# Both output projections and the down projection in seven half-size products with tokens stationary, the up projection in full products

## The chip, the cores and the metric

The kernel runs on one core of a Trainium2 chip. The metric is the device time of one execution in microseconds, here the median of three runs. A profile shows one further execution: its span is the time from its first to its last recorded instruction, and its own run time is a little longer. Line numbers (L385) are those of the kernel before, unless it is said that they are of the change.

## The reference

One decoder layer on 512 tokens of width 1024 with a memory of 256 tokens, all in float32. Three mixer branches (short convolution, stick-breaking attention, retention) are merged by gates; what the change touches is this:

```
merged = jnp.sum(gates * up, axis=2)
x = x + merged @ w_o[l]                      # 1024 x 1024
h = rmsnorm(x, norm_xa_g[l])
mem_n = rmsnorm(mem, norm_mem_g[l])
x = x + memory_attention(h, mem_n, w_xq[l], w_xkv[l], w_xo[l])   # ends in o @ w_out, 1024 x 1024
h = rmsnorm(x, norm_mlp_g[l])
x = x + squared_relu_mlp(h, w_up[l], w_down[l])                  # square(relu(h @ w_up)) @ w_down
return rmsnorm(x, final_g)
```

`w_up` is 1024 x 4096 and `w_down` 4096 x 1024.

## The kernel before, in words

**Numbers.** Every float32 operand is split in two parts, h (rounded) and l (the rest). A product is three matmuls that accumulate in PSUM: h by h, h by l, l by h (`mm3`, L234 to L236). `split` makes h on ScalarE (a cast) and l on VectorE (a subtraction); `parts_of` (L111, L112) does the same for a block of weights.

**Weights.** They come in blocks of 128 x 1024 (512 KB) on SyncE's DMA queue into `w_raw` (RAWS = 3 buffers), and their parts lie in `w_part` (WBUFS = 11 buffers). The class `Stream` loads and splits them in the order in which a list of items, `plan`, uses them, AHEAD = 2 steps before.

**Order of the work.** `run_plan` walks through `plan` and calls each item. The order of instructions on an engine is then set by the framework's list scheduler, which moves instructions between items as far as data, buffers and its own estimates allow; it is fixed when the kernel is built. On the chip each engine takes its instructions, and the DMAs that it issues, in that order. The loads of `x`, of the norm gains `g_bc` and of the memory rows `m_sb` are issued by ScalarE.

**PSUM.** Two pools of four banks: `mmps` (tag "mm") and `atps` (tag "at"). The transposes of a normed token tile (`norm_T`, L385: eight 128 x 128 in two "at" banks) use "at".

**Two kinds of product.** In `proj_t` the weights are stationary and 512 tokens stream; the result has channels in partitions. In `proj_m` the tokens are stationary and 512 weight columns stream; the result has tokens in partitions, so it can be added to `x`. `w_o`, `w_xo` and `w_down` go by `items_m`: two halves of 512 columns, four chunks of weights each, four token tiles in four "mm" banks; after the last chunk `add_x` (L836) adds each bank to `x`. This is 192 matmuls for `w_o`, 192 for `w_xo` and 768 for `w_down`, all 512 wide.

**Seven products.** `seven` (L290 to L308) multiplies 2 x 2 blocks with seven half-size products in place of eight (Winograd's form): sums and differences of weight blocks (`Seven.combo`, L137) and of token blocks (`Mixes`) are multiplied, and the products are added up. Here the weights are stationary and 256 tokens stream. It serves 12 of the 24 columns of gates and, of the up projection's 32 columns, all but the first U7 = 8: 12 pairs of columns with 84 matmuls 256 wide each.

**Stages around the change.** The gates of the third branch end in pairs of `seven`; each finished merged column is split into `mgs`. Then `reload_x` loads x again, `mem_norm` loads two tiles of memory, norms and transposes them (L354, L376, L385), and `proj_norm` runs `w_o`: first half of columns, then the second half token by token, with each token's norm (`norm_begin`, `norm_end`) and transposes behind its last sum. Keys and values of the memory follow, then cross-attention (`xa_scores`, `xa_transpose`, `xa_out`), whose result is split into `xo`; `proj_norm` runs `w_xo`; `first_up` starts the MLP. In four rounds `up7` makes eight columns of `u` and `items_m` multiplies them by 1024 rows of `w_down`. The last half of columns goes token by token, and `final` norms and stores each token tile (L1034).

```
pss[t] = mmps()
proj_m(pss[t], ws, a(), t, 0, 8)
...
dve.tensor_tensor(out=dst, in0=ps, in1=dst, op=ALU.add)
```

Of the kernel before, what the change touches and what calls it, by code (L numbers as in the profile page):

```python
# [33 lines left out]
RAWS, WBUFS, AHEAD = 3, 11, 2  # L34
G7, U7 = 12, 8
# [3 lines left out]
def trunk_kernel(ctx: ExitStack, tc: tile.TileContext, x, mem, par, rot, dqd, kdec, g_mix, g_xa, g_mem, g_mlp,  # L39
# [75 lines left out]
    class Plain:  # L115


        def __init__(self, t, c):
            self.loads = [(t, c)]
            self.steps = [lambda raw: parts_of(raw[0])]  # L120
            self.parts = []
# [3 lines left out]

    class Seven:


        def __init__(self, t, c):
            self.loads = [(t, c), (t, c + 1)]  # L130
            self.steps = [self.s0, self.s1, self.s2, self.s3]
            self.parts = []

        def combo(self, a0, a1, b0, b1):
            x = wpool.tile([P, CW], F32, name="w_mix", bufs=2)
            dve.tensor_tensor(out=x[:, :512], in0=a0, in1=a1, op=ALU.subtract)
            dve.tensor_tensor(out=x[:, 512:], in0=b0, in1=x[:, :512] if b1 is None else b1, op=ALU.subtract)  # L137
            return x
# [4 lines left out]
        def s1(self, raw):  # L143
            ra, rb = raw
            self.x1 = self.combo(ra[:, 512:], ra[:, :512], rb[:, :512], ra[:, 512:])
            return parts_of(self.x1)

        def s2(self, raw):
            rb = raw[1]
            return parts_of(self.combo(rb[:, :512], self.x1[:, :512], rb[:, 512:], None))  # L150
# [8 lines left out]

    class Stream:  # L160
        def __init__(self, entries):
            self.loads = [l for e in entries for l in e.loads]
            self.steps, first = [], 0
            for e in entries:
                e.first = first
                for i, st in enumerate(e.steps):
                    self.steps.append((e, st, first + (len(e.loads) if i else 1)))
                first += len(e.loads)
                e.last = len(self.steps)
# [33 lines left out]
    def run_plan():  # L203
        entries, index = [], {}
        for chunks, _ in plan:
            for kind, t, c in chunks:
# [6 lines left out]
        for chunks, fn in plan:  # L213
            es = [index[(t.tensor.name, c)] for _, t, c in chunks]
            if es:
                done = max([done] + [e.last for e in es])
                st.pump(done + AHEAD)
            fn(*[e.get() for e in es])
# [28 lines left out]

    class Mixes:
# [7 lines left out]
        def make(self, g):  # L256
# [13 lines left out]
            mix("S3", scr("mix", (P, 2, 256)), a11, a21, ALU.subtract)  # L270
            mix("S1", a21, a21, whole(4, 256), ALU.add)
            mix("S2", a11, a21, a11, ALU.subtract)
# [9 lines left out]
    def seven(b, a):  # L282
# [11 lines left out]
        s, u, y1, y2 = scr("sv_s"), scr("sv_u"), scr("sv_1"), scr("sv_2")  # L294
        lo, hi = slice(0, 256), slice(256, 512)
        prod(p1, "A11", "B11", True)
        act.copy(out=s[:, lo], in_=p1[:, lo])  # L297
        prod(p3, "S1", "T1", True)
        act.copy(out=s[:, hi], in_=p3[:, lo])
        prod(p1, "S2", "T2", False)  # L300
        act.copy(out=u[:, lo], in_=p1[:, lo])
        prod(p2, "A12", "B21", True)
        dve.tensor_tensor(out=y1[:, lo], in0=p2[:, lo], in1=s[:, lo], op=ALU.add)
        prod(p1, "S3", "T3", False)
        act.copy(out=u[:, hi], in_=p1[:, lo])
        dve.tensor_tensor(out=y2[:, hi], in0=s[:, hi], in1=u[:, hi], op=ALU.add)
        prod(p3, "S4", "B22", False)
        dve.tensor_tensor(out=y2[:, lo], in0=p3[:, lo], in1=u[:, lo], op=ALU.add)  # L308
        prod(p1, "A22", "T4", False)
        return y1, p1, y2  # L310
# [40 lines left out]
    def sumsq(src, c, ss, dst):  # L351

        cs = slice(c * 512, (c + 1) * 512)
        act.activation(out=dst[:, cs], in_=src[:, cs], func=AF.Square, accum_out=ss[:, c:c + 1])  # L354
# [7 lines left out]
    def norm_begin(key, src):  # L362
# [4 lines left out]
        sumsq(src, 0, ss, S["xn", key])  # L367
# [3 lines left out]
    def norm_end(key, src, g_bc):  # L371

        xn, ss = S["xn", key], S.pop(("ss", key))
        sumsq(src, 1, ss, xn)
# [347 lines left out]
    def gated(n, d, ps2, gt):  # L722
# [8 lines left out]
        if n == 2:  # L731
            if d % 2 == 0:
                S["mgs", d // 2] = [unit("mgs") for _ in range(2)]
            hi, lo = S["mgs", d // 2]
            split(hi[:, d % 2, :], lo[:, d % 2, :], m)
# [14 lines left out]
    def item_t7(fn, src, c, *chunks):  # L750

        def go(w, *ws):
            y1, p1, y2 = seven(w, S["mix"])
            fn(0, ((slice(0, 256), y1[:, :256]), (slice(256, 512), p1[:, :256])), *ws)
            fn(1, ((slice(0, 512), y2),), *ws)
# [86 lines left out]
    def proj_norm(src, a, g, after):  # L842


        items_m(src, 0, a, add_x(0))

        def begin():
            S["g"] = load_g(g)
            S["hT"] = Split("hT", KT)
            for t in range(NT):  # L850
                norm_begin(t, S["x"][t])
        item(begin)
        its = capture(lambda: items_m(src, 4, a, add_x(1), tok_outer=True))
        for t in range(NT):
            plan.extend(its[2 * t:2 * t + 2])
            item(lambda t=t: norm_end(t, S["x"][t], S["g"]))
            if t > 0:
                item(lambda t=t: norm_T(t - 1, S["hT"], t - 1))
        after(lambda: item(lambda: norm_T(NT - 1, S["hT"], NT - 1)))
# [23 lines left out]
    def kv_proj(last_T):  # L883
        for d in range(KT):
            item_t(xk_done(d), w_xk, d, a=lambda: S["mT"], sl=slice(0, MEM))
            if d == 3:
                last_T()
# [3 lines left out]
    mgs = lambda k: [t[:, k % 2, :] for t in S["mgs", k // 2]]  # L891
    proj_norm(w_o, lambda: mgs, g_xa, kv_proj)
# [44 lines left out]
    def xa_out(h):  # L937
        if h == 0:
            S["xo"] = Split("xo", KT)
        ph, pl = S.pop(("pT", h))  # L940
        for d in (2 * h, 2 * h + 1):
            ps = mmps()
            cs = slice(d * P, (d + 1) * P)
# [3 lines left out]
            hi, lo = S["xo"](d)  # L947
            split(hi, lo, ps)
# [16 lines left out]
    item(lambda: xa_out(3))  # L965


    def up_done(d):
        def fn(ps):
            if d == 0:  # L970
                S["u"] = Split("u", KT)
            r = scr("relu")
            act.activation(out=r, in_=ps, func=AF.Relu)
            dve.tensor_tensor(out=r, in0=r, in1=r, op=ALU.mult)
            hi, lo = S["u"](d)
            split(hi, lo, r)
        return fn

    def first_up(last_T):

        n, pss = 4, {}
        for half_ in range(2):
            for d in range(n):
# [8 lines left out]
                if half_ == 0 and d == 1:  # L992
                    last_T()
        mix = capture(mix_items)
        for i, d in enumerate(range(n, U7)):
            item_t(up_done(d), w_up, d)
            plan.extend(mix[i:i + 1])
        plan.extend(mix[U7 - n:])

    proj_norm(w_xo, lambda: S["xo"], g_mlp, first_up)  # L1000

    def up7(r):
        for q in range(U7 // 2 if r == 0 else 0, KT // 2):
            def fn(e, halves, q=q):
                d = 2 * q + e
                if d == 0:
                    S["u"] = Split("u", KT)
                r = scr("relu")
                for sl, src in halves:
                    act.activation(out=r[:, sl], in_=src, func=AF.Relu)  # L1010
                act.activation(out=r, in_=r, func=AF.Square)
                hi, lo = S["u"](d)
                split(hi, lo, r)
            item_t7(fn, w_up7, KT * r + 2 * q - U7)

    for r in range(4):
        up7(r)
        items_m(w_down, 8 * r, lambda: S["u"], add_x(0))
        if r < 3:
            items_m(w_down, 8 * r + 4, lambda: S["u"], add_x(1))  # L1020


    def final_begin():
        S["g"] = load_g(g_fin)
        for t in range(NT):
# [125 lines left out]
```

## Time and profile before

| | |
|---|---|
| median of 3 runs | 1033.91 us (1033.85 to 1033.92) |
| the profiled execution, its own time | 1033.71 us |
| its span | 1032.0 us |
| weight parts on VectorE (L112), of raw weights | 180 instructions, 210.9 us |
| weight parts on VectorE (L112), of mixed weights | 36 instructions, 44.0 us |
| weight parts on ScalarE (L111), of raw weights | 180 instructions, 180.6 us |
| HBM read, written | 103.31 MB, 2.10 MB |

The page splits the span into busy time per engine, follows back the chain of work that ended last, and groups instructions by line. A matmul's recorded time (0.39 us at 512 columns) overlaps the next one's; what it costs in a row of them is the distance between two starts. PE is TensorE, DVE VectorE, ACT ScalarE, POOL GpSimd, SP SyncE; a q behind the name (ACTq) is the engine's queue as it issues a DMA. A row of a timeline has start, duration, engine, line, operation, output<-inputs, shapes and a count, and in brackets how long the engine had been idle and what ended it.

### The profile page before, as it was taken

Reading aid. Unit: us, or ns where it says so; the run is one execution under the profiler, and the core shown is the slowest. Engines: PE = TensorE matmul, PEld = TensorE weight load, DVE = VectorE, ACT = ScalarE, POOL = GpSimd, SP = SyncE. Lnnn points to the kernel's source line nnn. Section 1 sums busy time; section 2 is a strip of 40 time slices with the busy share of each in tenths; the row PEclk is TensorE's granted clock in tenths of the full one; section 3 lists DMA queues with packets and bytes.
Section 4 is the critical chain, followed back from the end, with each engine's and each line's share of the span. In section 5 each row is a group of like instructions: output and inputs, shape, how many; then the busy total and the mean of one; then the engine's idle time right before and its main releaser. Section 6 shows DMA issues by size and latency. Waiting matters only on the chain.

```text
span 1032.0 us, 14325 instructions
## 1 busy us (share of the span) xinstructions
PE 1015.5 (98%) x5636; PEld 884.9 (86%) x5636; DVE 648.8 (63%) x992; ACT 500.7 (49%) x887; POOL 66.2 (6%) x118
## 2 busy tenths in 40 slices
PE   6999999999999999999999999999999999999997
PEld 4888888888888889998898888898889989989985
DVE  5567777856563796784584555466947566565643
ACT  6465567766532154463463444345416624643741
POOL 1101112321110000000100000000000000000000
PEclk9999999999999999999999999999999999999999
DMA  6322233213122212335354213223222321332222
GB/s 265 103 102 81 83 104 102 82 42 123 62 87 79 100 62 83 103 119 198 133 184 163 82 47 118 81 83 123 86 79 82 125 92 71 124 123 80 103 85 81
DMA packets 29876, 106.33 MB, mean 103 GB/s; under 512 B 3569, under 2 KB 3569, under 8 KB 29809
## 3 DMA queue, kind: packets, MB, share of 16 engines
q1 hardware_dynamic: 27216, 98.05, 27.7%
q10 hardware_dynamic: 2592, 7.37, 2.0%
q8 instruction: 44, 0.72, 0.3%
q14 instruction: 24, 0.19, 0.1%
HBM read 103.31 MB, written 2.10 MB: 102 GB/s over the span
## 4 chain that ended last, share of the span: by engine, by line
PE 97%; DMA 1%; DVE 0%; ACT 0%; SPq 0%; issue 0%; DVEq 0%; POOLq 0%; POOL 0%
PE mm L235 24%; PE mm L234 24%; PE mm L236 24%; PE p L290 17%; PE at L385 1%; PE o L546 1%; PE aT L512 1%; DMA w_raw<-in_w_in_dram 1%; PE z L488 1%; PE z L489 0%; PE xsc L236 0%; PE xsc L235 0%; PE xsc L234 0%; PE ro L693 0%; PE sc L667 0%; PE xpp L929 0%
## 5 line engine op out<-in xcount | busy, mean ns | idle before, releaser
L112 DVE TENSOR_TENSOR w_part<-w_raw,w_part 128x1024 fp32r<-128x1024 f32 (+1 forms) x180 | 210.9, 1176 | 168.1 <-PE mm L235 75.2
L111 ACT CAST w_part<-w_raw 128x1024 fp32r<-128x1024 f32 (+1 forms) x180 | 180.6, 1006 | 135.2 <-PE mm L236 79.1
L234 PE MATMUL mm<-hT_h,w_part 128*128 128x512 f32 (+1 forms) x512 | 193.6, 379 | 0.0
L235 PE MATMUL mm<-hT_l,w_part 128*128 128x512 f32 (+1 forms) x512 | 193.3, 378 | 0.0
L236 PE MATMUL mm<-hT_h,w_part 128*128 128x512 f32 (+1 forms) x512 | 193.0, 378 | 0.0
L290 PE MATMUL p<-mix_h,w_part 128*128 128x256 f32 x576 | 112.2, 283 | 0.5 <-ACT sv_s L297 0.5
L236 PEld LDWEIGHTS mm<-hT_h,w_part 128*128 128x128 f32 x512 | 96.4, 188 | 17.1
L234 PEld LDWEIGHTS mm<-hT_h,w_part 128*128 128x128 f32 x512 | 96.2, 188 | 16.8
L235 PEld LDWEIGHTS mm<-hT_l,w_part 128*128 128x128 f32 x512 | 96.5, 188 | 16.4
L235 PE MATMUL mm<-w_part,u_h 128*128 128x512 f32 x256 | 99.8, 390 | 0.0
L234 PE MATMUL mm<-w_part,u_h 128*128 128x512 f32 x256 | 98.6, 390 | 0.0
L236 PE MATMUL mm<-w_part,u_l 128*128 128x512 f32 x256 | 98.2, 389 | 0.0
L290 PEld LDWEIGHTS p<-mix_h,w_part 128*128 128x128 f32 x576 | 93.4, 192 | 1.4 <-ACT sv_s L297 0.7
L290 PE MATMUL p<-hT_h,w_part 128*128 128x256 f32 x432 | 84.4, 283 | 0.0
L290 PE MATMUL p<-mix_l,w_part 128*128 128x256 f32 x288 | 81.5, 283 | 0.0
L290 PEld LDWEIGHTS p<-hT_h,w_part 128*128 128x128 f32 x432 | 70.1, 192 | 0.8
L111 ACT CAST w_part<-w_mix 128x1024 fp32r<-128x1024 f32 x36 | 37.8, 1051 | 55.9 <-PE mm L235 37.5
L112 DVE TENSOR_TENSOR w_part<-w_mix,w_part 128x1024 fp32r<-128x1024 f32 x36 | 44.0, 1221 | 26.7 <-ACT w_part L111 20.0
L290 PE MATMUL p<-hT_l,w_part 128*128 128x256 f32 x216 | 60.7, 283 | 0.0
L236 PEld LDWEIGHTS mm<-w_part,u_l 128*128 128x128 f32 x256 | 48.1, 188 | 9.8
L235 PEld LDWEIGHTS mm<-w_part,u_h 128*128 128x128 f32 x256 | 48.1, 188 | 9.5
L234 PEld LDWEIGHTS mm<-w_part,u_h 128*128 128x128 f32 x256 | 47.9, 188 | 9.5
(211 smaller groups left out, 1813.2 us busy)
## 6 DMA issues: line engine op xcount, KB each, us to landing
w_raw<-in_w_in_dram SPq DMA_DIRECT2D x52, 512.0 KB, 3.4
w_raw<-in_w_up_dram SPq DMA_DIRECT2D x32, 512.0 KB, 3.6
w_raw<-in_w_down_dram SPq DMA_DIRECT2D x32, 512.0 KB, 3.4
w_raw<-in_w_br_dram SPq DMA_DIRECT2D x12, 512.0 KB, 3.4
w_raw<-in_w_gate_dram SPq DMA_DIRECT2D x12, 512.0 KB, 3.5
w_raw<-in_w_o_dram SPq DMA_DIRECT2D x8, 512.0 KB, 3.5
w_raw<-in_w_xk_dram SPq DMA_DIRECT2D x8, 512.0 KB, 4.2
w_raw<-in_w_xv_dram SPq DMA_DIRECT2D x8, 512.0 KB, 3.5
```

The costliest lines, as they stand in the source:

```text
L111: act.copy(out=wh, in_=src)
L112: dve.tensor_tensor(out=wl, in0=src, in1=wh.bitcast(F32), op=ALU.subtract)
L234: te.matmul(ps, lh, rh, start=first, stop=False)
L235: te.matmul(ps, lh, rl, start=False, stop=False)
L236: te.matmul(ps, ll, rh, start=False, stop=last)
L290: te.matmul(ps[:, :256], x[:, k, :], y, start=first and k == 0 and i == 0, stop=k == 3 and i == 2, skip_group_check=True)
L385: te.transpose(ps[:, k * P:(k + 1) * P], xn[:, c * P:(c + 1) * P], ident)
L488: te.matmul(z[:, :s], q[:, e, tsl], S["skh", hp][:, e, :s], start=True, stop=False)
L512: te.transpose(aps[:, sb * P:(sb + 1) * P], a[:, sb * P:(sb + 1) * P], ident)
L546: te.matmul(dst, vv, rhs, start=sb == 0 and i == 0, stop=sb == nblk and i == 1, skip_group_check=True)
```

## The change

- `w_o` and `w_xo` (`Wide1`) and `w_down` (`Wide2`, which takes twice as many rows per product) run by the new `items_w` in seven products with the tokens stationary and 512 columns streaming: 168, 168 and 672 matmuls. One `items_w` makes all 1024 output columns from 512 (`Wide1`) or 1024 (`Wide2`) rows of weights.
- The weight blocks of one such group (b11, b12, b22, b21) are mixed in place in `w_raw` by VectorE; products come in the order P1, P5, P6, P3, P2, P7, P4. P1 and P5 open sums in "at" banks, in which P6, P3, P7 and P4 go on; P2 has "mm" banks. After each product its sum is added to `x`; some products go on accumulating in the same bank and are added again: 14 adds per group, 112 in all, where there were 48.
- The token operands come from a new class `Pairs`: for each two columns of merged gates, attention output or squared ReLU, four differences by VectorE and four splits.
- The up projection runs in full products (`item_t`) for all 32 columns: 24 more columns of 24 matmuls 512 wide, and no pair of `seven`. Its `Mixes` go.
- `proj_norm` norms the tokens in two pairs: tokens 0 and 1 after P2, tokens 2 and 3 after P4 of the second group; `final` likewise.
- `seven` (for gates) is rewritten to mix weights in place and to return its results in the blocks that `Pairs` takes. RAWS goes from 3 to 6, WBUFS from 11 to 10.

```
+    class Wide:
+        def __init__(self, t, c):
+            nb = self.nb
+            self.loads = [(t, c + i) for i in range(4 * nb)]
+            self.steps = [lambda raw, n=n, j=j: self.step(raw, n, j) for n in range(7) for j in range(nb)]
...
+        def step(self, raw, n, j):
+            b11, b12, b22, b21 = (raw[m * self.nb + j] if m * self.nb + j < len(raw) else None for m in range(4))
+            if n == 1:
+                minus(b11, b12, b11)
+            elif n == 2:
+                plus(b11, b22, b11)
+                plus(b12, b12, b22)
+            elif n == 6:
+                minus(b11, b21, b11)
+            return parts_of((b11, b11, b11, b22, b21, b12, b11)[n])
...
+    class Pairs:
+        def make(self, e, s, u):
...
+            v = scr("pr_v", (P, 2, 256))
+            minus(v, u[:, 0:1, :].broadcast_to([P, 2, 256]), s)
+            put(("A11", "A22"), s)
+            minus(u[:, 0, :], s[:, 0, :], v[:, 1, :])
+            put(("S3", "S1"), v)
+            hi, lo = self.w[e]["A12"] = self.b[e // 2][:, e % 2, 0, :], self.b[e // 2][:, e % 2, 1, :]
+            split(hi, lo, u[:, 1, :])
+            minus(u[:, 1, :], u[:, 1, :], u[:, 0, :])
+            put(("S2", "S4"), u)
...
+    def items_w(kind, src, c, pairs, after=lambda p: None):
...
+                bank = dict(P2="p2", P5="p3", P3="p3").get(p, "p1")
+                if p in ("P1", "P5", "P2"):
+                    for i in range(2):
+                        acc[bank, i] = (mmps if p == "P2" else atps)(bank)
...
+                        for m, (x, y) in enumerate(((ah, wh), (ah, wl), (al, wh))):
+                            te.matmul(acc[bank, i], x, y, start=p in ("P1", "P5", "P2") and j + k + m == 0,
+                                      stop=j == nb - 1 and k == 1 and m == 2, skip_group_check=True)
...
+                    dve.tensor_tensor(out=dst, in0=acc[bank, i], in1=dst, op=ALU.add)
...
-    proj_norm(w_o, lambda: mgs, g_xa, kv_proj)
+    proj_norm(w_o, lambda i: S["mp", i], g_xa, lambda: None, kv_proj)
...
-        up7(r)
-        items_m(w_down, 8 * r, lambda: S["u"], add_x(0))
+    def down(r):
+        items_w(Wide2, w_down, 8 * r, lambda: S["u", r], last if r == NP // 4 - 1 else lambda p: None)
```

The order on the engines shifts in two places. The first is the start of the first output projection. TensorE before, where the transposes of the first memory tile (`at`) stand; `mm` are the projection's sums, `mgs` the merged gates:

```order
L234 MATMUL mm_4625<-w_part_4609,mgs_4350 128x512
L385 MATMUL at_4407<-ident_73,xn_4397 128x128 x4
L385 MATMUL at_4414<-ident_73,xn_4397 128x128 x4
L235 MATMUL mm_4625<-w_part_4610,mgs_4350 128x512
L236 MATMUL mm_4625<-w_part_4609,mgs_4351 128x512
L234 MATMUL mm_4657<-w_part_4513,mgs_3840 128x512
L235 MATMUL mm_4657<-w_part_4514,mgs_3840 128x512
```

Between the last matmul of `seven` and these transposes stand 101 matmuls of the projection. TensorE after the change, from the end of P2 of the first group on (`p2`, its input `pr_b` is A12), up to the first of P1:

```order
L403 MATMUL p2_4550<-w_part_4509,pr_b_3850 128x512
L403 MATMUL p2_4550<-w_part_4508,pr_b_3850 128x512
L499 MATMUL at_4426<-ident_73,xn_4416 128x128 x4
L499 MATMUL at_4433<-ident_73,xn_4416 128x128 x4
L499 MATMUL at_4452<-ident_73,xn_4442 128x128 x4
L499 MATMUL at_4459<-ident_73,xn_4442 128x128 x4
L403 MATMUL p1_4472<-w_part_4237,pr_3853 128x512
L403 MATMUL p1_4472<-w_part_4238,pr_3853 128x512
```

P2's 12 matmuls are all that stands between the last matmul of `seven` and the transposes of the first memory tile (`xn_4416`); those of the second tile (`xn_4442`) follow at once, and P1 comes behind both. ScalarE's queue at the same place, before:

```order
L111 CAST w_part_4543<-w_raw_4481 128x1024
L223 CAST mgs_4350<-mg_2984 128x512
L99 DMA x_4373<-in_x_dram 128x1024
L99 DMA x_4374<-in_x_dram 128x1024
L99 DMA x_4375<-in_x_dram 128x1024
L99 DMA x_4376<-in_x_dram 128x1024
L93 DMA g_bc_4389<-in_g_mem_dram 128x1024
L817 DMA m_sb_4395<-in_mem_dram 128x1024
L111 CAST w_part_4603<-w_raw_4511 128x1024
L111 CAST w_part_4609<-w_raw_4541 128x1024
L354 ACTIVATE xn_4397,ss_4398<-m_sb_4395 128x512 x2
```

And after the change:

```order
L265 CAST pr_4389<-mg_2990 128x512
L99 DMA x_4392<-in_x_dram 128x1024
L99 DMA x_4393<-in_x_dram 128x1024
L99 DMA x_4394<-in_x_dram 128x1024
L99 DMA x_4395<-in_x_dram 128x1024
L93 DMA g_bc_4408<-in_g_mem_dram 128x1024
L932 DMA m_sb_4414<-in_mem_dram 128x1024
L468 ACTIVATE xn_4416,ss_4417<-m_sb_4414 128x512 x2
L265 CAST mT_h_4410<-at_4426 128x4x128
L265 CAST mT_h_4411<-at_4433 128x4x128
L932 DMA m_sb_4440<-in_mem_dram 128x1024
```

The loads stand behind the last cast of the token mixes of the last two merged columns (`pr_4389`), where they stood behind the cast of the last merged column; that cast takes what VectorE's last mix leaves in `mg_2990`. On VectorE, 15 instructions stand between the add that takes S3's product of the last `seven` out of PSUM (before its last 12 matmuls may write there) and the end of that mix: 4 of 128x1024, 8 of 128x512 and 3 of 128x256, among them the gates' product of the last matmuls. The second memory tile's load stands behind the casts of the first tile's transposes, before (further down) as after.

The second place is the end of the second output projection, where the MLP's norm begins. TensorE before, around the first token's transposes (`at_6087`); `mm_6105` is the second token's sum:

```order
L236 MATMUL mm_6105<-w_part_5941,xo_l_5430 128x512
L385 MATMUL at_6087<-ident_73,xn_5983 128x128 x4
L385 MATMUL at_6096<-ident_73,xn_5983 128x128 x4
L234 MATMUL mm_6105<-w_part_6001,xo_h_5427 128x512
L235 MATMUL mm_6105<-w_part_6002,xo_h_5427 128x512
L236 MATMUL mm_6105<-w_part_6001,xo_l_5431 128x512
```

And after the change, from the end of P4 (`p1_6109`) to the first products of the up projection (`mm_6339`):

```order
L403 MATMUL p1_6109<-w_part_6200,pr_6089 128x512
L403 MATMUL p1_6109<-w_part_6199,pr_6089 128x512
L499 MATMUL at_6265<-ident_73,xn_6190 128x128 x4
L499 MATMUL at_6274<-ident_73,xn_6190 128x128 x4
L499 MATMUL at_6315<-ident_73,xn_6194 128x128 x4
L499 MATMUL at_6324<-ident_73,xn_6194 128x128 x4
L276 MATMUL mm_6339<-hT_h_6182,w_part_6239 128x256
L276 MATMUL mm_6370<-hT_h_6182,w_part_6285 128x256
L276 MATMUL mm_6419<-hT_h_6182,w_part_6335 128x256
L276 MATMUL mm_6468<-hT_h_6182,w_part_6366 128x256
L277 MATMUL mm_6339<-hT_l_6186,w_part_6239 128x256
```

The transposes of the first two tokens no longer lie among the projection's matmuls but behind the last of them. On VectorE, `xn_6190` comes behind both adds of P7, a weight part and the norm's small sums; the low part `hT_l_6186` behind `xn_6194`, both adds of P4, a weight part and the norm of the third token.

More of the change, by code (lines that the diff above doesn't have):

```diff
@@ L33 @@
 UNITS, SCRS = 30, 9
[L34 to L35 removed]
+RAWS, WBUFS, AHEAD = 6, 10, 2
+G7, UP = 12, 8
 @with_exitstack
```

283 lines of the change are left out of this document (169 added, 114 removed).

## The prediction

> **What bounds the kernel now.** I read the page first (engine totals, the chain that ended last), then TensorE's waits, then timelines of the stages that change.
>
> ```profile
> span 1032.0 us, 14325 instructions
> PE 1015.5 (98%) x5636; PEld 884.9 (86%) x5636; DVE 648.8 (63%) x992; ACT 500.7 (49%) x887; POOL 66.2 (6%) x118
> PE 97%; DMA 1%; DVE 0%; ACT 0%; SPq 0%; issue 0%; DVEq 0%; POOLq 0%; POOL 0%
> ```
>
> The chain is TensorE for 97% of the span. The next view lists all that TensorE waited for:
>
> ```profile
> PE at L385 <- DVE xn L376: 9.0, 2, 8.5
> PE p L290 <- ACT sv_s L297: 0.5, 1, 0.5
> ```
>
> 8.5 of these 9.5 us are the first norm of the kernel. So before, the time is the sum of the matmuls; any work removed from TensorE is gained in full, and any new wait is paid in full, because nothing else is waiting there now. The price of a 512-wide matmul comes from two rows of the down projection, 39 matmuls apart in the timeline; that of a 256-wide one from the row of the chain that groups 254 of them in the up projection.
>
> ```profile
> 922.16 0.39 PE L234 MATMUL mm<-w_part,u_h 128*128 128x512 f32 x1
> 931.00 0.39 PE L234 MATMUL mm<-w_part,u_h 128*128 128x512 f32 x1
> ...
> 942.72 30.47 PE p L290 x254
> ```
>
> (931.00 − 922.16)/39 = 0.2267 us; 30.47/254 = 0.120 us.
>
> **The matmuls.** Each output projection goes from 192 to 168 matmuls of width 512, the down projection from 768 to 672: 144 fewer, 144 × 0.2267 = **−32.6**. The up projection's 12 pairs of 84 matmuls of width 256 (1008 × 0.120 = 121.0) become 24 columns of 24 matmuls of width 512 (576 × 0.2267 = 130.6): **+9.6**. Together −23.0 us. This much is sure, and it is all that the change can win, as TensorE has no other wait to lose.
>
> **The entry to the first output projection.** T is the end of the last half-size gate product. Before, it is 477.73, from the first row, of the chain; the others are of ScalarE's queue, where the loads of x, g and memory are issued:
>
> ```profile
> 476.30 1.43 PE p L290 x12
> ```
> ```profile
> 476.33 0.62 ACT L223 CAST mgs<-mg 128x512 fp32r<-128x512 f32 x1 [1.49 <-DVE mg L730]
> ...
> 480.25 1.92 ACTq L99 DMA_DIRECT2D x<-in_x_dram  x4
> ...
> 483.09 0.33 ACTq L817 DMA_DIRECT2D m_sb<-in_mem_dram  x1
> ...
> 494.35 0.63 ACT L354 ACTIVATE xn<-m_sb 128x512 f32<-128x512 f32 x1 [6.39 <-DMA m_sb<-in_mem_dram]
> ...
> 501.58 0.34 ACTq L817 DMA_DIRECT2D m_sb<-in_mem_dram  x1
> ...
> 505.00 0.63 ACT L354 ACTIVATE xn<-m_sb 128x512 f32<-128x512 f32 x1 [2.79 <-DMA m_sb<-in_mem_dram]
> ```
>
> The x loads start at T+2.5, the first memory tile is asked for at T+5.4 and is only worked on at T+16.6. VectorE's and TensorE's timelines go on:
>
> ```profile
> 496.68 1.28 DVE L376 SCALAR_TENSOR_TENSOR xn<-m_sb,rstd,g_bc 128x1024 f32<-128x1024 f32 x1
> ...
> 508.09 1.28 DVE L376 SCALAR_TENSOR_TENSOR xn<-m_sb,rstd,g_bc 128x1024 f32<-128x1024 f32 x1
> ```
> ```profile
> 500.50 1.03 PE L385 MATMUL at<-ident,xn 128*128 128x128 f32 x8
> ```
>
> Before, nobody waits for this: 101 matmuls of the projection (22.9 us) stand in TensorE's queue ahead of the transposes. In the changed order there are only 12 (P2's), then both tiles' 16 transposes, then P1. P2's accumulators are in the pool of four "mm" banks, but P1's and P5's share the "at" banks with the transposes and come behind them. TensorE takes its queue in order, so all of P1, P5, P6, P3 waits for memory rows that are not in SBUF.
>
> The loads also start later. In ScalarE's queue they now follow the last cast of the token mixes, which needs VectorE's last mix. The add that releases TensorE's last 12 matmuls ends at T−1.4, and behind it VectorE has 4 instructions of 1024, 8 of 512 and 3 of 256 before that mix is done. Their prices, as distances between starts:
>
> ```profile
> 447.49 0.68 DVE L729 TENSOR_TENSOR gt<-mm,gt 128x512 f32<-128x512 f32 x1
> 448.09 0.68 DVE L137 TENSOR_TENSOR w_mix<-w_raw,w_mix 128x512 f32<-128x512 f32 x1
> 448.69 1.22 DVE L112 TENSOR_TENSOR w_part<-w_mix,w_part 128x1024 fp32r<-128x1024 f32 x1
> 449.82 0.68 DVE L730 TENSOR_TENSOR mg<-mg,gt 128x512 f32<-128x512 f32 x1
> 450.42 0.41 DVE L303 TENSOR_TENSOR sv<-p,sv_s 128x256 f32<-128x256 f32 x1
> 450.76 0.41 DVE L308 TENSOR_TENSOR sv<-p,sv_u 128x256 f32<-128x256 f32 x1
> ```
>
> 1.13, 0.60 and 0.34: 4.5 + 4.8 + 1.0 = 10.3, so T+8.9; a cast of 0.6 (the row at 476.33), and x is asked for at T+9.5, the memory tile 2.84 later (483.09 − 480.25) at T+12.4. It lands at best T+19: six loads of 0.5 MB from T+9.5 at the rate of this row, 3.15 MB / 412 = 7.6, and 2 for the first to start.
>
> ```profile
> 490.00:492.00 2.00, 2.00 (x11) 1.65 (x10) 1.60 (x2) 0.00 (x0) 0.00 (x0) 1.00 1.02 412
> ```
>
> At worst it takes the 11.3 of before (494.35 − 483.09): T+23.7. I take T+21.5. From there to the end of xn are 3.6 (497.96 − 494.35): T+25.1. The second tile can only be asked for after the first one's transposes, since its DMA is queued on ScalarE behind the casts of them: from the first transposes to the second xn were 8.9 (509.37 − 500.50), 8.1 without VectorE's other work (505.00 + 3.6 − 500.50); I take 8.5, T+33.6, and 0.8 for its transposes. P1 starts at T+34.4 with 4.3 of work done (12 × 0.2267 + 2 × 0.8): **+30**, between 27 and 33.
>
> [...]
>
> **The clock after it.** After 8.5 us of idling at the start, TensorE runs slowly at first:
>
> ```profile
> 8.47 1.94 PE L385 MATMUL at<-ident,xn 128*128 128x128 f32 x8 [8.47 <-DVE xn L376]
> 10.53 0.79 PE L234 MATMUL mm<-w_part,hT_h 128*128 128x512 f32 x1
> ...
> 16.26 0.39 PE L234 MATMUL mm<-w_part,hT_h 128*128 128x512 f32 x1
> 16.49 0.40 PE L235 MATMUL mm<-w_part,hT_h 128*128 128x512 f32 x1
> ...
> 18.55 1.10 PE L385 MATMUL at<-ident,xn 128*128 128x128 f32 x8 [0.51 <-DVE xn L376]
> ```
>
> 12 matmuls took 16.26 − 10.53 = 5.7 instead of 2.7. The wait above is longer, so P1 begins this way: **+3** (0, if the transposes in between keep it quick, to 4).
>
> **The entry to the MLP.** Before, the transposes of each token tile lay between products of the next. In the new order the eight-transpose groups of tokens 0 and 1 and the first up products follow the last product P4 directly, and xn of token 0 waits on VectorE behind the adds of P7 and a weight part. From P7's add of the first token (t): the add of the second by t+2.0, a weight part of 1.13, xn's small sums and power, xn (1.28) by t+5.7; then the P4 add and the second xn, t+7.6; transposes of it to t+8.4; the low parts of hT wait for one more add, weight part and xn and come at about t+11.5. TensorE's own work ends P4 at t+4.1, and 2.6 of transposes and first products lie in the gap: 11.5 − 4.1 − 2.6 = 4.8, **+5** (3 to 7). The kernel's last rows show these links at its end, where nothing covers them:
>
> ```profile
> 1025.24 0.69 DVE L836 TENSOR_TENSOR x<-mm,x 128x512 f32<-128x512 f32 x1 [1.66 <-PE mm L236]
> 1025.97 0.63 ACT L354 ACTIVATE xn<-x 128x512 f32<-128x512 f32 x1 [4.71 <-DVE x L836]
> 1026.72 0.16 DVE L358 SCALAR_TENSOR_TENSOR ms<-ss 128x1 f32<-128x1 f32 x1 [0.79 <-ACT xn L354]
> 1027.03 0.55 POOL L348 TENSOR_TENSOR rstd<-ms,half 128x1 f32<-128x1 f32 x1 [4.89 <-DVE ms L358]
> 1027.61 1.41 DVE L1034 SCALAR_TENSOR_TENSOR xn<-x,rstd,g_bc 128x512 f32<-128x512 f32 x2 [0.73 <-POOL rstd L348]
> ```
>
> After so short a gap I count +1 for the clock, between 0 (if it acts as the 0.5 us wait at 18.55, after which the transposes took 1.10, not 1.94) and 3 (the start). [...]
>
> **VectorE in the projections.** One column group of an output projection needs 7 weight parts and 4 mixes of 1024 and 14 adds of 512: 11 × 1.13 + 14 × 0.60 = 20.8, against 84 × 0.2267 = 19.0 on TensorE: 1.8 short, 7.2 in four groups. For w_o the stall hides it (VectorE has its parts ready). At w_xo it comes behind softmax and token mixes, where nothing does: **+3**, between 0 and 7. A column group of the down projection has 14 parts, 8 mixes and 14 adds, 33.3 against 38.1: hidden, as are the token mixes of gates and up. **+1** for places where they bunch (0 to 3). ScalarE's added casts, copies and squares cost nothing: it is busy for 49% of the span, and each of them has a product's length on TensorE to hide in; without that cover a cast of 0.6 would be paid per product. The weights' bytes and loads stay as many, with six raw buffers for three. **Tail:** the last add is followed by the chain quoted, now for two tokens, one behind the other's writes: **+1** (0 to 1.5).
>
> **Sum.** 1033.7 for the profiled run (span 1032.0; the median of 1033.9 is the same within 0.2) − 23.0 + 30 + 3 + 5 + 1 + 3 + 1 + 1 = 1054.7: **1055**. All low ends: 1033.7 − 23 + 27 + 0 + 3 = 1041; all high ends: 1033.7 − 23 + 33 + 4 + 7 + 3 + 7 + 3 + 1.5 = 1069.
>
> **Rivals.** *The memory rows come in time* (the other side): the loads have no data to wait for but the reuse of buffers; if ScalarE's queue reached them before T, the entry and its clock would cost nothing, 1055 − 33 = **1022**, faster. The stall decides at about 10 us: P1 would have to start at T+14, so the first tile to be there before T+1 and asked for by about T−9. For it: before, ScalarE was nearly idle there. Against: the order of its queue, with the cast ahead. 6%.
> *VectorE bounds every group*: parts mixed in place must be made in turn, and if adds delay parts at each product, the 7.2 of four groups is paid whole, with some 3 at the gates and 3 in the MLP: 1055 − 3 − 1 + 13 = **1064**. For it: the 20.8 above 19.0. Against: ten buffers of parts, which let it run ahead. 15%.
> *The MLP's entry and w_xo are covered*: the norm of tokens 0 and 1 begins after P2, and P7 and P4 (24 × 0.2267 = 5.4) are longer than its chain of 2.4 (1027.61 − 1025.24), so that the entry's 5 and 1 and w_xo's 3 vanish: 1055 − 9 = **1046**. For it: that chain. Against: VectorE's order, with the adds and parts ahead of xn. 14%.
>
> **How the numbers follow.** The forecast's own case has 65%. 0.2% (2 us) is about what a measurement of this kernel can tell from no change. Faster is the first rival, 6%; 2% is left for a time in between that comes out level; slower 92%. The range runs from just above the low ends to just below the high ones, and takes in the second and third rival: 1042 to 1067.
>
> **What would show it.** In the profile after: TensorE's waits name the memory norm's transposes on VectorE's xn with some 25 to 30 us in two waits, and the slices around 480 to 510 us drop on PE; the x loads are issued 9 to 10 us after the last gate product, not 2.5; a second group of waits of about 5 us at the first up products. TensorE's busy time less its cold matmuls falls by about 23. I am wrong if the transposes are not waited for, or if w_o's and w_xo's products wait on VectorE's parts by more than 7 us.

## The result, and the profile after

The changed kernel takes 1065.24 us (median of 4 runs, 1064.96 to 1065.43) against 1033.88 us before: a ratio of 1.0303, 95% interval 1.0285 to 1.0321. It is slower by 31.4 us; forecast were 1055, range 1042 to 1067. One execution of e8 below, of 2038 us, is left out of its median as a slow one; all other executions count. The head of the page of the profile after:

```profile
span 1062.8 us, 13386 instructions
...
PE 1005.8 (95%) x5060; PEld 851.7 (80%) x5060; DVE 752.3 (71%) x1120; ACT 529.4 (50%) x935; POOL 65.4 (6%) x118
...
PEclk9999999999999999996799999999999999999999
...
PE 87%; DVE 8%; DMA 2%; issue 1%; ACT 1%; POOL 0%; SPq 0%; ACTq 0%; DVEq 0%; POOLq 0%
```

TensorE's share of the chain went from 97% to 87%; VectorE, absent before, has 8%. The granted clock, at 9 tenths everywhere before, dips in the slices from 478 to 531 us. TensorE's busy time fell by only 9.7 us, not by the 23.0 of the removed matmuls, for the most part since it works for 20.4 us at a granted clock of 0.50 (3.3, 7.0, 3.3, 3.4 and 3.4 us in the five stretches that the last section lists). What TensorE waits for, the largest groups of its waits (us in total, times, longest):

```profile
PE at L499 <- DVE xn L490: 32.9, 5, 15.5
PE p L403 <- DVE x L409: 4.0, 3, 3.5
PE at L499 <- DVE hT_l L266: 3.1, 2, 2.7
PE p L403 <- DVE w_part L112: 3.1, 2, 2.9
PE p L403 <- ACT w_part L111: 1.6, 1, 1.6
PE p L334 <- DVE sv_s L348: 1.5, 1, 1.5
PE mm L277 <- DVE hT_l L266: 1.3, 1, 1.3
```

L499 are the transposes of a normed tile, L403 the seven products with tokens stationary, L409 the adds to x, L490 the end of a norm. The first group had 9.0 before, of which 8.5 are the start of the kernel. Where the new ones lie, in TensorE's timeline (start, duration, and in brackets the idle time and what ended it):

```profile
475.55 0.39 PE L334 MATMUL p<-hT_h,w_part 128*128 128x256 f32 x1 [1.49 <-DVE sv_s L348]
478.83 0.73 PE L403 MATMUL p<-w_part,pr_b 128*128 128x512 f32 x2 [1.58 <-ACT w_part L111]
482.48 4.08 PE L403 MATMUL p<-w_part,pr_b 128*128 128x512 f32 x10 [2.92 <-DVE w_part L112]
502.02 1.94 PE L499 MATMUL at<-ident,xn 128*128 128x128 f32 x8 [15.46 <-DVE xn L490]
511.40 1.94 PE L499 MATMUL at<-ident,xn 128*128 128x128 f32 x8 [7.44 <-DVE xn L490]
...
566.35 1.06 PE L499 MATMUL at<-ident,xn 128*128 128x128 f32 x8 [2.75 <-DVE hT_l L266]
567.78 1.97 PE L499 MATMUL at<-ident,xn 128*128 128x128 f32 x8 [0.37 <-DVE hT_l L266]
...
714.45 4.57 PE L403 MATMUL p<-w_part,pr 128*128 128x512 f32 x12 [3.52 <-DVE x L409]
720.30 1.30 PE L499 MATMUL at<-ident,xn 128*128 128x128 f32 x8 [0.41 <-DVE ms L472]
721.89 0.73 PE L276 MATMUL mm<-hT_h,w_part 128*128 128x256 f32 x4 [0.29 <-ACT hT_h L265]
723.94 0.38 PE L277 MATMUL mm<-hT_l,w_part 128*128 128x256 f32 x1 [1.31 <-DVE hT_l L266]
```

There are three places: the entry to the first output projection (478 to 513), where both memory tiles' transposes wait one after the other, 15.5 and 7.4 us; the entry to keys and values (563 to 568), where the transposes of a later token tile wait for the split of an earlier one's; and the last product of w_xo with the first of the up projection (711 to 724). Behind them the same work takes longer: 8 transposes 1.94 where they took 1.03, 12 matmuls 4.57 where 12 x 0.2267 + 0.16 = 2.9 is their time at a granted clock of 1.00.

ScalarE's timeline at the first place shows the loads:

```profile
486.65 0.82 ACTq L99 DMA_DIRECT2D x<-in_x_dram  x2
487.31 0.61 ACT L265 CAST pr<-mg 128x512 fp32r<-128x512 f32 x1
487.50 0.94 ACTq L99 DMA_DIRECT2D x<-in_x_dram  x2
...
489.00 0.50 ACTq L932 DMA_DIRECT2D m_sb<-in_mem_dram  x1
498.32 0.63 ACT L468 ACTIVATE xn<-m_sb 128x512 f32<-128x512 f32 x1 [10.40 <-DMA m_sb<-in_mem_dram]
...
504.00 0.33 ACTq L932 DMA_DIRECT2D m_sb<-in_mem_dram  x1
507.70 0.63 ACT L468 ACTIVATE xn<-m_sb 128x512 f32<-128x512 f32 x1 [3.12 <-DMA m_sb<-in_mem_dram]
```

The last product of the gates ends at T = 477.1: the row at 475.55 begins its 12 matmuls, the last one starts at 476.97 and costs 0.12. (By the end of its record, which the forecast went by, T is 477.25, and every distance from T is smaller by 0.15.) The loads of x are issued from T+9.5 on, when VectorE's last mix has ended (486.61) and before the last cast of the token mixes runs (487.31); the first memory tile is asked for at T+11.9 and ScalarE takes it up at T+21.2; the second is asked for behind the first one's transposes.

### The profile page after: what moved, and what is told of

Its sections match the earlier page's. It is cut to its first block, busy times and chain, and to the rows that moved or that the text cites. A ratio compares the mean times of both kernels' runs of the same rounds, so it can differ in the third digit from the quotient of the medians.

```text
span 1062.8 us, 13386 instructions
## 1 busy us (share of the span) xinstructions
PE 1005.8 (95%) x5060; PEld 851.7 (80%) x5060; DVE 752.3 (71%) x1120; ACT 529.4 (50%) x935; POOL 65.4 (6%) x118
## 4 chain that ended last, share of the span: by engine, by line
PE 87%; DVE 8%; DMA 2%; issue 1%; ACT 1%; POOL 0%; SPq 0%; ACTq 0%; DVEq 0%; POOLq 0%
PE mm L277 19%; PE mm L278 19%; PE mm L276 19%; PE p L403 18%; PE p L334 4%; DVE w_part L112 2%; DVE x L409 2%; DMA m_sb<-in_mem_dram 1%; PE at L499 1%; PE o L660 1%; PE aT L626 1%; DVE xn L490 1%; DMA w_raw<-in_w_in_dram 1%; PE z L602 1%; PE z L603 0%
## 5 line engine op out<-in xcount | busy, mean ns | idle before, releaser
L112 DVE TENSOR_TENSOR w_part<-w_raw,w_part 128x1024 fp32r<-128x1024 f32 (+1 forms) x228 | 274.7, 1207 | 155.3 <-ACT w_part L111 141.0
L277 PE MATMUL mm<-hT_l,w_part 128*128 128x512 f32 (+1 forms) x704 | 269.0, 382 | 1.3 <-DVE hT_l L266 1.3
L278 PE MATMUL mm<-hT_h,w_part 128*128 128x512 f32 (+1 forms) x704 | 268.9, 382 | 0.0
L276 PE MATMUL mm<-hT_h,w_part 128*128 128x512 f32 (+1 forms) x704 | 268.1, 383 | 0.3 <-ACT hT_h L265 0.3
L403 PE MATMUL p<-w_part,pr 128*128 128x512 f32 x864 | 205.1, 395 | 4.1 <-DVE x L409 4.0
L403 PEld LDWEIGHTS p<-w_part,pr 128*128 128x128 f32 x864 | 163.8, 191 | 39.9 <-ACT xn L468 3.9
L278 PEld LDWEIGHTS mm<-hT_h,w_part 128*128 128x128 f32 x704 | 133.2, 189 | 24.7
L276 PEld LDWEIGHTS mm<-hT_h,w_part 128*128 128x128 f32 x704 | 132.5, 189 | 24.3 <-ACT hT_h L265 0.5
L409 DVE TENSOR_TENSOR x<-p,x 128x512 f32<-128x512 f32 x112 | 74.8, 683 | 15.6 <-PE p L403 15.3
L499 PE MATMUL at<-ident,xn 128*128 128x128 f32 x112 | 18.8, 317 | 36.4 <-DVE xn L490 32.9
L499 PEld LDWEIGHTS at<-ident,xn 128*128 128x128 f32 x112 | 15.1, 164 | 39.1 <-issue 36.4
L403 PE MATMUL p<-w_part,pr_b 128*128 128x512 f32 x144 | 36.8, 404 | 4.7 <-DVE w_part L112 3.1
L127 DVE TENSOR_TENSOR w_raw<-w_raw 128x1024 f32<-128x1024 f32 (+1 forms) x36 | 37.5, 1042 | 1.0 <-DMA w_raw<-in_w_down_dram 0.5
L130 DVE TENSOR_TENSOR w_raw<-w_raw 128x1024 f32<-128x1024 f32 (+1 forms) x36 | 37.4, 1040 | 0.2
L403 PEld LDWEIGHTS p<-w_part,pr_b 128*128 128x128 f32 x144 | 27.9, 196 | 11.6 <-DVE w_part L112 4.0
L334 PE MATMUL p<-mix_h,w_part 128*128 128x256 f32 x192 | 36.8, 283 | 0.0
L334 PEld LDWEIGHTS p<-mix_h,w_part 128*128 128x128 f32 x192 | 30.9, 192 | 0.2
```

The costliest lines, as they stand in the source:

```text
L112: dve.tensor_tensor(out=wl, in0=src, in1=wh.bitcast(F32), op=ALU.subtract)
L127: dve.tensor_tensor(out=out, in0=a, in1=b, op=ALU.subtract)
L130: dve.tensor_tensor(out=out, in0=a, in1=b, op=ALU.add)
L276: te.matmul(ps, lh, rh, start=first, stop=False)
L277: te.matmul(ps, lh, rl, start=False, stop=False)
L278: te.matmul(ps, ll, rh, start=False, stop=last)
```

## The experiments

| run | what it does | us (median) | ratio to before, interval |
|---|---|---|---|
| changed kernel | | 1065.24 | 1.0303 (1.0285 to 1.0321) |
| e1 | memory loads early | 1051.71 | 1.0175 (1.0160 to 1.0191) |
| e2 | memory transposes in "mm" banks | 1046.10 | 1.0117 (1.0102 to 1.0132) |
| e9 | memory norm behind w_o's first group | 1046.47 | 1.0122 (1.0105 to 1.0139) |
| e3 | e2 and all loads early | 1041.71 | 1.0086 (1.0069 to 1.0103) |
| e8 | e3 without w_o's mixes | 1032.91 | 0.9992 (0.9983 to 1.0002) |
| e4 | without w_xo's mixes | 1057.55 | 1.0232 (1.0217 to 1.0248) |
| e5 | w_xo undone | 1057.66 | 1.0232 (1.0215 to 1.0249) |
| e6 | w_o undone | 1030.39 | 0.9965 (0.9952 to 0.9978) |
| e7 | w_o and w_xo undone | 1023.33 | 0.9901 (0.9886 to 0.9915) |

**e1: the memory rows early.** The loads of the memory norm become an item of their own ahead of the last gates.

```
+    def mem_load():
+        S["gm"] = load_g(g_mem)
+        S["msb"] = [unit("m_sb", (P, D), F32) for _ in range(2)]
+        for t in range(2):
+            act.dma_start(out=S["msb"][t], in_=mem[t * P:(t + 1) * P, :])
...
+    item(mem_load)
     gates7(2, "rt", range(KT // 2))
```

> The memory rows and their norm gain are loaded before the last gates; the order on TensorE stays, both memory tiles' transposes ahead of P1. Theory (the transposes stand ahead of P1, and their rows come late): the load's own part of the wait goes, but the memory norm's squares still stand behind the last token mix on ScalarE, about 10 us after the last gate product, and the second tile's behind the first one's transposes: P1 starts about 22 us after that product, not 36, and the time falls by about 14 to 1051 (1047 to 1055). Rival (the transposes do not hold TensorE, it waits for weight parts or token mixes): no change, 1065. Rival (the load is all of it): 1033 or less.

It took 1051.71, 13.5 less. TensorE's timeline of e1 at the entry:

```profile
493.25 1.94 PE L499 MATMUL at<-ident,xn 128*128 128x128 f32 x8 [5.15 <-DVE xn L490]
499.40 1.94 PE L499 MATMUL at<-ident,xn 128*128 128x128 f32 x8 [4.21 <-DVE xn L490]
500.99 4.35 PE L403 MATMUL p<-w_part,pr 128*128 128x512 f32 x15
```

The rows are asked for ahead of the last gates, and the transposes still hold P1 up to 501 (waits of 5.15 and 4.21 us for VectorE's xn), since the norm's squares and sums stand behind the token mixes. So the load is 13.5 of the entry's cost and not all of it.

**e2 and e9: the order, not the load.** e2 gives the memory transposes another bank pool; e9 leaves the banks and moves one item.

```
-            norm_T(t, S["mT"], t)
+            norm_T(t, S["mT"], t, mmps)
```
```
-    item(mem_norm)
-    proj_norm(w_o, lambda i: S["mp", i], g_xa, lambda: None, kv_proj)
+    proj_norm(w_o, lambda i: S["mp", i], g_xa, lambda: item(mem_norm), kv_proj)
```

> Only the bank pool of the two memory tiles' transposes is changed, from at to mm, the loads stay late. Theory: P1, P5 and the others go ahead of the transposes, some 66 matmuls after the last gate product, so TensorE no longer waits for memory rows; but P1's bank can only be used on after its first add to x, and x is asked for 10 us late, so a wait of about 12 us for the x rows takes its place: the time falls by about 18 to 1047 (1042 to 1052). If the late x does not matter: 1032. If bank sharing is not the cause: 1065.

> Only the place of the memory norm in the code changes: after w_o's first column group instead of ahead of it; loads as late as in the change, transposes in at banks. Theory (it is the order in which the at banks are given out that puts the transposes ahead of P1, not the sharing as such): as e2, the wait for x takes the place of the wait for memory: 1046 (1042 to 1050). Rival (sharing as such holds P1): 1060 or more.

They took 1046.10 and 1046.47. TensorE's timeline of e2, and then VectorE's at the same place:

```profile
493.07 15.31 PE L403 MATMUL p<-w_part,pr 128*128 128x512 f32 x60 [11.26 <-DVE x L409]
520.64 1.94 PE L499 MATMUL mm<-ident,xn 128*128 128x128 f32 x8 [4.00 <-DVE xn L490]
```
```profile
492.32 0.69 DVE L409 TENSOR_TENSOR x<-p,x 128x512 f32<-128x512 f32 x1 [2.13 <-DMA x<-in_x_dram]
```

P1 now runs ahead of the memory norm, and 11.3 us of another wait stand there: P1's bank goes on accumulating only after its first sum was added to x, and x is asked for late too, in e2 at 488.86. In e9 the same wait has 12.0 us. Two different edits with one effect show that the order in which the "at" banks are handed out put the transposes ahead of P1; sharing the pool does no harm by itself. They give 19 us back and not the whole entry, since the late x takes the place of the late memory rows.

**e3 and e8: everything early, and VectorE behind it.** e3 joins e1's and e2's edits and also loads x ahead of the last gates. e8 takes from it the in-place mixes of w_o's weights.

> Memory rows, norm gain and x are loaded before the last gates, and the memory transposes use mm banks. Theory: both causes of the wait at the first output projection are gone, with the cold clock behind it: the time falls by about 33 to 1032 (1029 to 1037), the wait of TensorE for the memory norm is below 3 us. Rival (the vector engine cannot make parts, token mixes and adds at that place in time): a new wait of 5 to 10 us there, 1038 to 1043.

> As e3 (memory rows and x early, memory transposes in mm banks), and the in-place mixes of w_o's weights are left out, 8 x 1.13 = 9.0 us of VectorE work (so everything behind w_o differs). Theory (in e3 VectorE works without a gap from 478 to 513 and is what TensorE's waits of 10.9 us between 486 and 517 come from): 6 to 9 us less than e3, 1034 (1032 to 1037). Rival (the memory norm's own chain through ScalarE sets the last wait): 1040 to 1042.

e3 took 1041.71: the theory's 1032 missed, the rival's 1038 to 1043 right. The busy times of e3 in a stretch behind the gates (its length, then PE, PEld, DVE, ACT, POOL with their instructions, granted clock, DMA share, GB/s), and TensorE's last wait at this place in e3 and then in e8:

```profile
478.00:513.00 35.00, 27.96 (x116) 21.15 (x116) 34.44 (x47) 18.82 (x30) 0.56 (x1) 0.95 0.28 92
```
```profile
516.92 1.49 PE L499 MATMUL mm<-ident,xn 128*128 128x128 f32 x8 [4.50 <-DVE xn L490]
```
```profile
509.45 1.94 PE L504 MATMUL mm<-ident,xn 128*128 128x128 f32 x8 [4.36 <-DVE xn L495]
```

VectorE works for 34.4 of 35 us in e3: token mixes of the last gates, weight parts, mixes and adds of w_o and the memory norm all fall together there. 9.0 us of it taken away gave 8.8 us (1032.91), and the second memory tile's transposes come 7.5 us earlier. With the loads cured, VectorE's work sets the time at this place; in the changed kernel that was hidden inside the longer wait for the load. The rival's wait for the memory norm is there too: the last wait stays at 4.4 us in e8.

**e4: VectorE at w_xo.** The four mixes of each of w_xo's groups are left out.

```
+    class Raw1(Wide1):
+        def step(self, raw, n, j):
+            m = (0, 1, 2, 2, 3, 1, 0)[n]
+            return parts_of(raw[m])
```

> The four in-place mixes of each column group of w_xo are left out, 8 x 1.13 = 9.0 us of VectorE work (so x after cross-attention is wrong); all else as in the change. Theory (VectorE is late from 680 to 715, and TensorE's 3.5 us wait for the add at P4 and the slow clock after it come from that): 6 to 8 us less, 1058 (1056 to 1060). Rival (the wait is the chain of adds and banks, whatever VectorE does): 1064 to 1066.

1057.55, 7.7 less, as the theory had it. The stretch before w_xo's last product, of the changed kernel and then of e4:

```profile
680.00:715.00 35.00, 30.97 (x133) 24.71 (x132) 35.00 (x49) 18.19 (x31) 0.00 (x0) 0.99 0.36 119
```
```profile
680.00:715.00 35.00, 32.58 (x149) 26.41 (x148) 34.28 (x53) 20.92 (x37) 3.61 (x3) 1.00 0.47 151
```

VectorE has no gap at all in the first (in the second TensorE gets further in the same stretch, 149 matmuls for 133), and the wait of 3.52 us ahead of the last product became 0.70:

```profile
708.83 2.98 PE L408 MATMUL p<-w_part,pr 128*128 128x512 f32 x12 [0.70 <-DVE ss L487]
```

**e5, e6 and e7: one part at a time undone.** w_xo, w_o, or both go back to `items_m` with split operands as before; all the rest stays.

```
-    proj_norm(w_xo, lambda i: S["xo", i], g_mlp, lambda: item(lambda: xa_out(3)), first_up)
+    proj_norm_m(w_xo, lambda: S["xo"], g_mlp, first_up)
```
```
-    proj_norm(w_o, lambda i: S["mp", i], g_xa, lambda: None, kv_proj)
+    proj_norm_m(w_o, lambda: mgs, g_xa, kv_proj)
```

> Only w_xo goes back to full products (24 matmuls more, 5.4 us); w_o, w_down and up stay changed. Theory: the 6 us lost at w_xo (waits for adds, slow clock) and the 3.5 us at the first up products go, as norms and transposes lie among the matmuls again: 1065 + 5.4 - 9.5 = 1061 (1059 to 1063). Rival (the MLP's entry stalls because of the new up projection, not of w_xo): 1065 + 5.4 - 6 = 1064.

> Only w_o goes back to full products with split merged gates (24 matmuls more, 5.4 us); w_xo, w_down and up stay changed, and so do the order of loads in the code and the six raw buffers. Theory: 33 us of the first output projection's entry, 2 to 3 at the gates' end and 5 to 6 at the entry to keys and values go: 1065 + 5.4 - 41 = 1029 (1026 to 1033), faster than before. Rival (the load of memory and x is late for another reason, buffers or the queues): 1045 or more.

> w_o and w_xo both go back to full products; only w_down in seven products and the up projection in full ones stay. Theory: 96 matmuls fewer and up's 9.6 us, so 1033.7 - 21.8 + 9.6 = 1021.5, and 2 to 4 us of losses (tail 1, vector engine late at up and down): 1025 (1022 to 1027), the fastest of all. Rival (mixes in place and 14 adds per group make VectorE late in the MLP as in w_xo): 1030 or more.

e5 took 1057.66, below its range, e6 1030.39 and e7 1023.33, both within. Each undone projection costs 24 matmuls, 5.4 us, and takes its losses away. So w_o's were 1065.24 - 1030.39 + 5.4 = 40.3 us and w_xo's 1065.24 - 1057.66 + 5.4 = 13.0, or 12.5 from e6 and e7. What is left in e7 is 1023.33 - (1033.75 - 96 x 0.2267 + 9.6) = 1.7. The page of e7, and the only TensorE waits that it has:

```profile
PE 1003.3 (98%) x5108; PEld 853.2 (84%) x5108; DVE 682.7 (67%) x1012; ACT 505.9 (50%) x891; POOL 62.8 (6%) x118
```
```profile
PE at L499 <- DVE xn L490: 9.4, 3, 8.1
PE mm L276 <- ACT hT_h L265: 0.5, 1, 0.5
PE mm L276 <- ACT w_part L111: 0.3, 1, 0.3
```

This is the picture of before again: TensorE at 98%, and its one long wait the 8.1 us at the start. The down projection in seven products keeps what it saves. The likely reason is the prediction's own sum: each of its products has 24 matmuls, twice as many as w_o's, so a group has 33.3 us of work on VectorE under 38.1 on TensorE, where w_o has 20.8 against 19.0. No run tests this reason alone. e7 is the fastest version run, 10.4 us below before. The rival, VectorE late in the MLP as well, is refuted.

## Why the prediction was right, point by point

**The matmuls.** The -23.0 held as far as it was tested: e7 has 96 of the 144 matmuls and all of the up projection's change in it, and comes out within 1.7 us of the sum. For the other 48 matmuls the price is taken over, and the losses of w_o and w_xo are worked out with it; so 1033.75 - 23.0 + 40.3 + 12.5 + 1.7 = 1065.3 must close, and proves nothing more.

**The entry to the first output projection** was forecast step by step, and the steps are in the trace: x asked for at T+9.5 (forecast T+9.5), the first memory tile at T+11.9 (T+12.4), its squares at T+21.2 (T+21.5), its transposes at T+24.9 (T+25.1), the second one's at T+34.3 (T+33.6), P1 at T+35.9 (T+34.4, the row at 512.99 below). The two tiles' transposes took 1.94 each at a granted clock of 0.50, not the 0.8 between starts that was priced; that is the difference at P1. 35.9 - 4.3 = 31.6 us for the forecast 30. That x was asked for at just T+9.5 is partly luck: the last mix ended at T+9.5 and not T+8.9, as VectorE also waited 0.5 for ScalarE, and the cast of 0.6 that was added is not waited for. The 2 us that the forecast gave the first load to start stand in no row; in the run the first tile was taken up 9.3 us after it was asked for (498.32 - 489.00). The two waits for the memory norm are 15.5 + 7.4 = 22.9 us, less than the 25 to 30 that the prediction looked for: 4.5 us more of the entry went to waits for weight parts ahead of P2's matmuls.

**The clock after it** was priced 3 and cost 1.8: P1 begins at the lower clock for a part of its first 32 matmuls only,

```profile
512.99 9.19 PE L403 MATMUL p<-w_part,pr 128*128 128x512 f32 x32
```

(9.19 - 0.16)/32 = 0.282 against 0.2267, where 0.16 is how far a matmul's record goes past the next one's start. At a granted clock of 0.50 that is 3.5 us of work; the trace has 0.50 from 489.17 to 516.48 and 1.00 from there on. Whether the transposes in between had a part in this is not shown: at the kernel's start they came first too, and there the matmuls lost 3 us. How long the clock stayed low each time is told in the last section.

**What was missed at w_o.** e6 puts w_o's whole loss at 40.3, the two terms above are 33.4. The rest are the entry to keys and values, for which there was no term: 3.1 us of waits at 566 and 568, and a granted clock of 0.91 in the stretch around them, 19 x 0.09 = 1.7 us more,

```profile
554.00:573.00 19.00, 15.88 (x122) 15.47 (x121) 16.99 (x32) 11.17 (x28) 4.67 (x4) 0.91 0.42 143
```

and waits of 1.9 us ahead of T (0.42 at 461 for a part from ScalarE and 1.49 at 475.55 for VectorE), where VectorE has parts, mixes and token mixes at once; the term "where they bunch" had 1 for it. The step that failed is "for w_o the stall hides it" as a statement on the whole stage: it hid VectorE's shortage in w_o's products (the stretch from 514 to 554 has no wait), but neither at the end of the gates ahead of the stall nor at the norm behind the products.

**w_xo and the MLP's entry** were priced 3 + 5 + 1 = 9; undoing w_xo gives 12.5 to 13.0. Both mechanisms were there, in other sizes. e4 puts 7.7 of it on the 9.0 us of mixes, where 3 was priced: VectorE's shortage was the mis-sized term. Its lateness comes out mainly at one point, ahead of the last product: 2.8 us of the wait (3.52 - 0.70) and 1.6 of slow clock behind it (4.57 - 2.98). What e4 leaves, 12.5 - 7.7 = 4.8, is close to the 5 + 1 of the entry, but in the changed kernel the waits behind the last product, where the prediction had put 5, are only 0.41 + 0.29 + 1.31 = 2.0: the longer wait had come before that product, not at the first up products.

**Tail and the rest.** The last row of TensorE after:

```profile
1043.99 11.06 PE L403 MATMUL p<-w_part,pr 128*128 128x512 f32 x48
```

From its end to the end of the span are 1062.8 - 1055.05 = 7.8, before 1032.0 - 1025.2 = 6.8: +1.0, as forecast.

**The rivals.** The memory rows did not come in time. "VectorE bounds every group" gave 1064 and lies nearest to the measured time, but by another sum: it needed w_o's groups to be late throughout and the entry to be the same, and the trace has no wait in w_o's groups from P1 on. Its mechanism is not absent, though: e3 and e8 show that VectorE is short there once the stall is gone. "The MLP's entry and w_xo are covered" is refuted by e5. The forecast case holds, with its 44 us of losses measured as 54.5: 6 more at w_o, 5 of them at keys and values, 3.5 more at w_xo, and 0.7 in the rest.

**What stays open.** How much of the 40.3 is due to which of the three gates' end, entry and keys and values is read from waits and clock of one profile, not from runs that undo one of them alone; some 1 to 2 us of it and of the 12.5 are in no wait that the profile names. Whether the long products are what spares the down projection is argued, not tested.

## What to carry to other kernels

A change that saves work on the bounding engine can lose more through the order of that engine's queue (here 23.0 us saved, 40.3 lost at w_o alone): look first for what now stands ahead of the first new instruction, whose data that is, and where its load is queued. Accumulators in a shared bank pool took their turn here in the order in which the code asks for banks (e9, which only moves the memory norm, gave 18.8 us), so an item that waits for a load belongs behind the products it does not feed. A scheme that trades TensorE's work for VectorE's paid here in the down projection, with 24 matmuls a product, and lost where VectorE had more work than TensorE; apply it stage by stage, and measure each stage alone.

## What the runs showed of the hardware that had not been expected

Behind a wait of the same length, the same 12 matmuls, the last product of w_xo, took different times from run to run. In the changed kernel it is the row at 714.45 above; TensorE's timeline of e1, e2 and e3, one row each:

```profile
701.00 5.46 PE L403 MATMUL p<-w_part,pr 128*128 128x512 f32 x12 [3.52 <-DVE x L409]
```
```profile
695.78 3.01 PE L403 MATMUL p<-w_part,pr 128*128 128x512 f32 x12 [3.53 <-DVE x L409]
```
```profile
692.36 5.46 PE L403 MATMUL p<-w_part,pr 128*128 128x512 f32 x12 [3.51 <-DVE x L409]
```

At the price of 0.2267 they take 12 x 0.2267 + 0.16 = 2.9: in e2 nothing was lost, in e1 and e3 2.6 us, in the changed kernel 1.7. One kernel differs from itself too: e2's execution in the profile took 1044.44 us at a mean clock of 0.992, its other three 1045.88 to 1046.58 at 0.987. Shorter waits cost as much in places: behind the 2.92 us at 482.48 ten matmuls took 4.08 where 2.43 is their price, and a wait of 2.75 us, at 566.35, was followed by transposes of 1.06 and then, after 0.37 more, by others of 1.97. So the clock cost of waits of some 2.5 to 4 us could not be foretold here. The waits of 4.00 us and more that stand in the timelines, up to 15.46, all had a cost: behind them 8 transposes took 1.94, in e3 1.49, where they took 1.03; the 60 matmuls of e2 took 15.31 where 13.8 is their price.

The trace's record of the granted clock shows where the changed kernel lost it. Between 14.8 and 1059.1 the clock was 0.50 in five stretches and 1.00 outside them (the length, TensorE's busy time with its matmuls, granted clock, DMA share, GB/s):

```profile
14.80:482.34 467.54, 459.68 (x2439) 1.00 0.26 91
482.34:485.75 3.41, 3.27 (x8) 0.50 0.78 272
485.75:489.17 3.42, 0.81 (x4) 1.00 0.44 139
489.17:516.48 27.31, 7.02 (x24) 0.50 0.41 156
516.48:567.67 51.19, 48.19 (x269) 1.00 0.40 137
567.67:571.09 3.42, 3.31 (x16) 0.50 0.27 104
571.09:714.45 143.36, 139.08 (x711) 1.00 0.28 95
714.45:717.86 3.41, 3.41 (x8) 0.50 0.79 258
717.86:724.69 6.83, 4.78 (x31) 1.00 0.38 124
724.69:728.10 3.41, 3.41 (x18) 0.50 0.02 7
728.10:1059.10 331.00, 326.84 (x1528) 1.00 0.27 91
```

Four of the low stretches last 3.41 us and one 27.31, 8 times as long; their beginnings lie 6.83, 85.33, 232.11 and 242.35 us behind the first one's, 2, 25, 68 and 71 times 3.413. So in this run the clock changed only at whole multiples of 3.413 us from its first change, also in the midst of a row of matmuls without a wait, as at 516.48 in P1's 32. The means over 20 us of the other runs fit that length: 0.63 and 0.94 from 480 to 520 in e1 are (0.37 + 0.06) x 20 / 0.5 = 17.2 us at 0.50, 5.0 times 3.413; 0.74 from 480 to 500 in e2 is 10.4 us, 3.0 times; 0.85 and 0.98 from 500 to 540 in e3 are 6.8 us, 2.0 times. That the loss depends on how a wait lies to these changes is the author's estimate; no run moves a wait alone. The changed kernel's wait from 710.93 to 714.45 ends at one of them, and the 3.3 us behind it have half the clock (columns as for e3):

```profile
711.10:714.40 3.30, 0.00 (x0) 0.00 (x0) 3.30 (x5) 2.60 (x8) 0.00 (x0) 1.00 0.83 267
714.50:717.80 3.30, 3.30 (x8) 2.62 (x9) 2.64 (x9) 1.17 (x4) 1.07 (x2) 0.50 0.79 259
```

3.41 us of work at half the clock lose 3.41 / 2 = 1.7 us, which is the loss of the 12 matmuls there (4.57 - 2.9). Why the wait of 3.53 us in e2 cost nothing is not shown. How much waiting is enough stays open too: in the 3.41 us ahead of the low stretch at 724.69, at a clock of 1.00, TensorE waited for 0.29 + 1.31 = 1.6 us.
